# GpSimd makes one of four weight sums and the activation sums for the down projection, and two more feed-forward blocks go by seven products

## The chip, the cores and the metric

The kernel runs on one core of a Trainium2 chip. The metric is the device time of one execution in microseconds (us), less being better. The engines of the core are called here as the profile calls them: PE (TensorE, matrix products), DVE (VectorE), ACT (ScalarE), POOL (GpSimd) and SP (SyncE, whose queue issues most of the loads).

## The reference

One encoder layer over 512 tokens of width 1024, in float32: a mixer of two attention head groups, cross-attention into 256 memory tokens, and a SwiGLU feed-forward network (FFN). Only the FFN is touched:

```python
def swiglu(h, w_gate_up, w_down):
    g, u = jnp.split(h @ w_gate_up, 2, axis=-1)
    return (jax.nn.silu(g) * u) @ w_down
...
    h = rms_norm(x, g_ffn_pre[l])
    x = x + rms_norm(swiglu(h, w_gate_up[l], w_down[l]), g_ffn_post[l])
```

Here `h` is 512 x 1024, `w_gate_up` is 1024 x 5632 and `w_down` is 2816 x 1024.

## The kernel before

Every float32 matrix is split into a high part (a cast to the format `F32R` that PE takes) and a low part (the rest), and a product is made of three matmuls: high x high, high x low, low x high. Each weight tile therefore costs a cast on ACT (for weights of the FFN line 924) and a subtraction on DVE (line 925), both before PE can use it.

**Gate and up.** The 5632 columns of `w_gate_up` are 22 blocks of 256, `n` = 0 to 21. An even `n` is the gate of hidden pair `u = n // 2`, an odd one the up of the same pair. Blocks 0 and 1 use weights loaded early. A later block is a 2 x 2 arrangement of 512 x 512 by 512 x 128 quarters, and is made in one of two ways:

- by eight products (`eight_weights`, `eight`): two loads of 512 KB, `lower` and `upper`, each split; 96 matmuls of 256 columns; one evacuation per half.
- by seven products after Winograd (`seven_weights`, `seven`): 84 matmuls. The weights need four sums `s1` to `s4` of quarters (each 128 x 512), and 3.5 split tiles of 1024 in place of 2. The results come out of PSUM by five additions on DVE (lines 1161 to 1171), and for an up block two multiplications with the gate follow (lines 1181, 1183).

The split weights of a block are four items (a11; `s2`,`s4`; the raw `upper` quarters; `s3`,`s1`) in a ring in SBUF, which holds three slots of 1024 columns, so DVE and ACT prepare a block about one block ahead of PE. The raw loads have three buffers, `sums` two. Lines 951 to 954 make the sums. `EIGHT` names the blocks that go by eight.

Loads, casts, sums and evacuations stand in program order with priorities, and a scheduler in the build orders the instructions of each engine; the chip then runs each engine's queue in that order, with semaphores between engines.

**Products of the activations.** By seven products the activations need sums too, made once at the start (`f11`, `f12`, `f21`, `f22`; lines 1138 to 1142, split at 1134 and 1135 into `t1` to `t4`). Line 887 makes the low part of the activations' second half, on which the last matmuls of blocks 0 and 1 wait.

**Down.** `w_down` is taken in two column halves, in pairs `i` of 256 rows. Pairs 0 to 3 and 9, 10 are plain; pairs 4 to 8 (`SEVEN`) go by seven products, and `late_seven` makes their activation operands: first the raw quarters are split (`put`, lines 1217 and 1218), then four sums in place (lines 1222 to 1225, each 128 x 256), then the sums are split. The weights of these pairs are summed on DVE at lines 1001 to 1003.

An instruction whose two inputs both lie in SBUF is called a two-SBUF instruction below (lines 925, 951 to 954, 1222 to 1225 are such); lines 1161 to 1171 read one input from PSUM.

Of the kernel before, what the change touches and what calls it, by code (L numbers as in the profile page):

```python
# [11 lines left out]
ALU = mybir.AluOpType  # L12
AX = mybir.AxisListType

P = 128
# [21 lines left out]
def hybrid_block_kernel(  # L37
# [20 lines left out]
    act, dve, pool, pe = nc.scalar, nc.vector, nc.gpsimd, nc.tensor  # L58
# [12 lines left out]
    def f32(ap):  # L71
        return ap.bitcast(F32)
# [158 lines left out]
    with tc.tile_pool(name="mix", bufs=1, reuse_waits="tile") as bp:  # L231
# [126 lines left out]
        for t in range(NT):  # L358
# [3 lines left out]
                out=z[:, t, :], in0=acc0[t][:, 256:264], scalar=r, in1=gn[:, B_F : B_F + 8],  # L362
# [299 lines left out]
    with tc.tile_pool(name="cross", bufs=1, reuse_waits="tile") as cp:  # L662
# [20 lines left out]
        with later(-115):  # L683
            for c in range(4):
                hi, lo = unit()
                acc = bank("a")
                for b in range(2):
# [9 lines left out]
                    out=kT[:, 1, 2 * c : 2 * c + 2, :], in0=a3,  # L697
                    in1=f32(kT[:, 0, 2 * c : 2 * c + 2, :]), op=ALU.subtract,
# [7 lines left out]
        for half in range(2):  # L706
            hi, lo = unit()
            for t in range(NT):
                acc = bank("a")
                for k in range(4):  # L710
# [5 lines left out]
                    out=m, in0=acc, scalar=rs_g[1][:, t : t + 1], in1=m, op0=ALU.mult, op1=ALU.add  # L716
# [3 lines left out]
                if half:  # L720
                    r = small(1, "prs")
                    dve.scalar_tensor_tensor(
                        out=r, in0=mix_ms[:, 0, t : t + 1], scalar=EPS, in1=mix_ms[:, 1, t : t + 1],
# [4 lines left out]
                        out=mix[:, t, :], in0=mix[:, t, :], scalar=r, in1=xo[t], op0=ALU.mult, op1=ALU.add  # L728
# [39 lines left out]
        for h in range(4):  # L768
            hi, lo = unit()
            q = qq[:, h % 2]  # L770
            for b in range(2):
                acc = bank("a")
                cs = slice(b * P, (b + 1) * P)
                for k in range(KB):
# [3 lines left out]
                    out=q[:, 1, b, :], in0=acc, scalar=1.0 / 16.0, in1=f32(q[:, 0, b, :]),  # L778
# [3 lines left out]
            for i in range(0, NT, 2):  # L782
                s = bank("s")
                for j in range(2):
# [8 lines left out]
                    out=nm, in_=s.rearrange("p (j n) -> p j n", j=2), axis=AX.X, op=ALU.max, negate=True  # L793
# [9 lines left out]
                for j in range(2):  # L803
                    dve.tensor_scalar(
                        out=p[:, i + j, :], in0=p[:, i + j, :], scalar1=rs[:, j : j + 1],
# [11 lines left out]
            for b in range(2):  # L817
                acc = bank("o")
                cs = slice((2 * h + b) * P, (2 * h + b + 1) * P)
                for k in range(2):  # L820
# [6 lines left out]
                    out=oTl[2 * h + b], in0=acc, in1=f32(oTh[2 * h + b]), op=ALU.subtract  # L827
# [68 lines left out]
        def load_raw(w, k0, nkb, c0, ncol):  # L896
            raws[0] += 1
            raw = wp.tile([P, nkb, ncol], F32, tag="raw", name=f"fraw{raws[0]}", bufs=3)
            nc.sync.dma_start(
                raw, w[k0 * P : (k0 + nkb) * P, c0 : c0 + ncol].rearrange("(k p) n -> p k n", p=P)  # L900
            )
            return raw
# [13 lines left out]
        def item(at, size, fill):  # L916
            items.append((at, at + size, fill))

        def fill_from(at, shape, src, order=None):
            def fill():  # L920
                h, l = split(at, None, shape)
                h2, l2 = (a.rearrange(order) for a in (h, l)) if order else (h, l)
                v = src()
                act.copy(h2, v)  # L924
                dve.tensor_tensor(out=l2, in0=v, in1=f32(h2), op=ALU.subtract)  # L925
                return h, l

            return fill
# [3 lines left out]
        def single():  # L932
            nslot[0] += 1
            return AS_WEIGHTS + 512 * (nslot[0] % 2)

        def double():
            nslot[1] += 1
            return AS_WEIGHTS + 1024 + 1024 * (nslot[1] % 3)

        def seven_weights(n, c0):  # L940
            raw, total = {}, sums[:, n % 2]
            s2, s4, s3, s1 = (total[:, i] for i in range(4))

            def a11():
                raw["lower"] = load_raw(w_gate_up, 0, 4, c0, 256)
                raw["upper"] = load_raw(w_gate_up, 4, 4, c0, 256)
                return raw["lower"][:, :, :P]

            def s2_s4():
                lower, upper = raw["lower"], raw["upper"]  # L950
                dve.tensor_tensor(out=s1, in0=lower[:, :, P:], in1=upper[:, :, P:], op=ALU.add)
                dve.tensor_tensor(out=s2, in0=s1, in1=lower[:, :, :P], op=ALU.add)
                dve.tensor_tensor(out=s4, in0=s2, in1=upper[:, :, :P], op=ALU.add)
                dve.tensor_tensor(out=s3, in0=lower[:, :, :P], in1=lower[:, :, P:], op=ALU.add)
                return total[:, 0:2]

            two = dict(c=2, k=4, n=P)
            item(at := single(), 512, fill_from(at, dict(k=4, n=P), a11))
            item(at := double(), 1024, fill_from(at, two, s2_s4))
            item(at := double(), 1024, fill_from(at, two, lambda: raw["upper"], "p c k n -> p k c n"))  # L960
            item(at := double(), 1024, fill_from(at, two, lambda: total[:, 2:4]))
# [5 lines left out]
                    fill_from(at, dict(k=4, n=256), lambda k0=k0: load_raw(w_gate_up, k0, 4, c0, 256)),  # L967
                )

        EIGHT = (2, 3, 11)  # L970
        for n in range(2, FB):
            (eight_weights if n in EIGHT else seven_weights)(n, (n % 2) * FF + (n // 2) * 256)

# [67 lines left out]
        def hidden(u):  # L1041

            if u == 0:
                return G
            if u < 4 or u == 10:
                return U.rearrange("p t b n -> p b t n")
            if u in (4, 8):
                tag, size = {4: ("vm", 4160), 8: ("pt", 2112)}[u]
                gf.append(cp.tile([P, size], F32, tag=tag, name=f"gf{u}"))
            at = (u % 4 if u < 8 else u % 2) * 1024  # L1050
            return gf[-1][:, at : at + 1024].rearrange("p (b t n) -> p b t n", b=2, t=2)
# [53 lines left out]
        def up_eight(dst):  # L1105
            def done(m, acc):
                dve.tensor_tensor(out=dst[:, m], in0=G[:, :, m], in1=halves(acc), op=ALU.mult)

            return done

        def eight(tags, done, parts):
            accs = [bank(tag) for tag in tags]
            for half, bs in enumerate(((b11, b12), (b21, b22))):
                ((h, l),) = take()
                for m in range(2):
                    w = [a[:, :, m * P : (m + 1) * P] for a in (h, l)]
                    for n, ns in enumerate((left, right)):
                        begin = half == 0 and n == 0
                        product(accs[m][:, ns], w, bs[n], begin, half == 1 and n == 1, WHOLE if m or n or not half else parts)
                    if half:  # L1120
                        done(m, accs[m])
# [67 lines left out]
        for u in range(1, FB // 2):  # L1189
            parts = IN_STEP if u in (1, 2, 4, 6, 8, 10) else WHOLE  # L1190
            if 2 * u in EIGHT:
                eight(("a", "a"), gate_eight, parts)
            else:
                seven(G, ("a", "a", "a", "o"), gate_seven, parts)
            dst = hidden(u)
            if 2 * u + 1 in EIGHT:
                eight(("s", "s"), up_eight(dst), WHOLE)
# [13 lines left out]
        def late_seven(u):  # L1211

            h, l = late7[u]
            f = gf_views[u].rearrange("p (c n) -> p c n", n=256)

            def put(d, a):
                act.copy(h[:, d], f[:, a])
                dve.tensor_tensor(out=l[:, d], in0=f[:, a], in1=f32(h[:, d]), op=ALU.subtract)

            put(slice(0, 1), slice(0, 1))  # L1220
            put(slice(1, 3), slice(2, 4))
            dve.tensor_tensor(out=f[:, 3], in0=f[:, 1], in1=f[:, 3], op=ALU.add)
            dve.tensor_tensor(out=f[:, 1], in0=f[:, 0], in1=f[:, 1], op=ALU.subtract)
            dve.tensor_tensor(out=f[:, 0], in0=f[:, 3], in1=f[:, 0], op=ALU.subtract)
            dve.tensor_tensor(out=f[:, 2], in0=f[:, 2], in1=f[:, 0], op=ALU.subtract)
            put(slice(3, 7), slice(0, 4))

        gh, gl = ({(k if k < 8 else k + 12): a for k, a in enumerate(g)} for g in (gh, gl))
# [22 lines left out]
        for half, tail in enumerate((2, 3)):  # L1251
# [64 lines left out]
            for i in body:  # L1316
                if i in SEVEN:
                    if half == 0 and i == SEVEN[0]:
                        cuts.append(P)
                    seven_products(i, i == SEVEN[-1])  # L1320
                    if half == 0 and i == SEVEN[0]:
                        spare = cp.tile([P, 4160], F32R, tag="vm", name="latev")
                        copied = cp.tile([P, 1024], F32, tag="xp", name="f8", bufs=2)
                        act.copy(copied, gf_views[8])
                        gf_views[8] = copied
                        late(9, spare)
                        at = 2048 + AS_WEIGHTS
                        lows = cp.tile([P, 2112], F32R, tag="pt", name="latep")[:, AS_WEIGHTS:]
                        late7[8] = tuple(
                            a.rearrange("p (c n) -> p c n", n=256) for a in (spare[:, at : at + 1792], lows[:, :1792])  # L1330
                        )
                        late_seven(8)
                        gb3 = cp.tile([P, D], F32, tag="xp", name="gb3", bufs=2)
                        spare3 = cp.tile([P, D], F32, tag="xp", name="spare3", bufs=2)
                        junk3, gained = spare3[:, :512], spare3[:, 512:]
                        nc.gpsimd.dma_start(gb3, bcast(g_ffn_post))
                    if i == SEVEN[-1]:
                        gather()
                    continue
# [96 lines left out]
```

## Time and profile before

| | |
|---|---|
| runs | 774.8, 774.9 and 775.59 us, median 774.9 |
| profiled execution | span 771.6 us; its own time outside the profiler is not listed beside it, and the 3.3 us to the median lie around the span |
| PE busy | 755.6 us, 98% |
| DVE busy | 600.3 us, 78% |
| ACT busy | 429.4 us, 56% |
| POOL busy | 62.5 us, 8% |
| gate and up, blocks by seven or eight | about 442 to 649 us |
| down | about 649 to 766 us |

Busy time is the time during which at least one instruction of an engine runs. PE's matmuls overlap one another, so its pace is read from the starts of its instructions, not from their durations. The same holds in a small way for DVE, whose next instruction starts some 0.09 us before the end of the one before is recorded.

### The profile page before, as it was taken

To read this page: it belongs to the slowest core of one execution; us is meant where nothing else is said; L and a number is where in the kernel's file an instruction comes from. 1 tells how busy PE (TensorE), PEld (TensorE's weight loads), DVE (VectorE), ACT (ScalarE), POOL (GpSimd) and SP (SyncE) were. 2 spreads that over 40 slices of the span, in tenths; PEclk is the share of its full clock that TensorE was granted. 3 is DMA by queue.
4 is the path that set the end of the run, shared out by engine and by line. 5 is a ranking of instruction groups with operands and counts; after the bars stand their busy time and mean duration, and the time that the engine had idled before them with its cause. 6 is when DMAs were issued, how large, how long until landed. Compare 5 with 4: busy or idle time off the path is not lost.

```text
span 771.6 us, 12900 instructions
## 1 busy us (share of the span) xinstructions
PE 755.6 (98%) x5012; PEld 677.0 (88%) x5012; DVE 600.3 (78%) x1098; ACT 429.4 (56%) x784; POOL 62.5 (8%) x105
## 2 busy tenths in 40 slices
PE   9999999999999999999999999999999999999996
PEld 9977888887778988877778999999999999898985
DVE  8668889789886688545653779999899998987746
ACT  7558889567874457444553625554444446553421
POOL 1001132100321210000002100000000000000001
PEclk9999999999999999999999999999999999999999
DMA  7522023422313725311340202332433332233312
GB/s 273 139 70 68 28 56 97 123 82 82 109 56 112 267 98 197 120 54 56 131 143 27 83 28 83 110 110 82 138 110 110 110 110 90 102 112 108 106 59 109
DMA packets 60749, 80.05 MB, mean 104 GB/s; under 512 B 2705, under 2 KB 43665, under 8 KB 60689
## 3 DMA queue, kind: packets, MB, share of 16 engines
q1 hardware_dynamic: 59264, 74.49, 29.9%
q0 software_dynamic: 1280, 4.72, 1.7%
q8 instruction: 39, 0.64, 0.3%
q14 instruction: 22, 0.17, 0.1%
q10 hardware_dynamic: 144, 0.02, 0.0%
HBM read 77.13 MB, written 2.10 MB: 103 GB/s over the span
## 4 chain that ended last, share of the span: by engine, by line
PE 79%; DVE 9%; ACT 6%; issue 3%; DMA 2%; POOL 1%; DVEq 0%; POOLq 0%; ACTq 0%
PE ps_a L144 12%; PE ps_a L146 12%; PE ps_a L143 12%; PE ps_a L1094 3%; PE ps_a L1097 3%; PE ps_a L1095 3%; PE ps_s L1097 3%; PE ps_s L1094 3%; PE ps_s L1095 3%; PE ps_s L143 2%; PE ps_s L144 2%; PE ps_s L146 2%; PE ps_t L552 2%; PE ps_o L561 2%; PE ps_s L533 1%
## 5 line engine op out<-in xcount | busy, mean ns | idle before, releaser
L924 ACT CAST ring_hi<-fraw 128x1024 fp32r<-128x1024 f32 (+1 forms) x62 | 57.2, 932 | 61.0 <-DVE fraw L1003 17.0
L126 DVE TENSOR_TENSOR lo<-raw,hi 128x1024 fp32r<-128x1024 f32 x56 | 68.2, 1224 | 20.5 <-ACT hi L125 20.3
L925 DVE TENSOR_TENSOR ring_lo<-fraw,ring_hi 128x1024 fp32r<-128x1024 f32 (+1 forms) x62 | 66.5, 1075 | 17.4 <-ACT ring_hi L924 17.1
L146 PE MATMUL ps_a<-hTh,lo 128*128 128x512 f32 x192 | 76.6, 399 | 0.0
L144 PE MATMUL ps_a<-hTl,hi 128*128 128x512 f32 x192 | 75.9, 395 | 0.0
L143 PE MATMUL ps_a<-hTh,hi 128*128 128x512 f32 x192 | 75.8, 395 | 0.0
L125 ACT CAST hi<-raw 128x1024 fp32r<-128x1024 f32 x56 | 57.8, 1048 | 25.3 <-PE ps_a L144 21.2
L924 ACT CAST ring_hi<-sums 128x1024 fp32r<-128x1024 f32 x34 | 35.7, 1049 | 35.5 <-PE ps_t L1095 10.2
L925 DVE TENSOR_TENSOR ring_lo<-sums,ring_hi 128x1024 fp32r<-128x1024 f32 x34 | 41.4, 1219 | 2.1 <-ACT ring_hi L924 2.1
L144 PEld LDWEIGHTS ps_a<-hTl,hi 128*128 128x128 f32 x192 | 36.1, 188 | 6.4
L146 PEld LDWEIGHTS ps_a<-hTh,lo 128*128 128x128 f32 x192 | 36.1, 188 | 6.3
L143 PEld LDWEIGHTS ps_a<-hTh,hi 128*128 128x128 f32 x192 | 36.2, 188 | 5.7
L547 ACT ACTIVATE p<-p,nm 128x128 f32<-128x128 f32 (+1 forms) x64 | 36.1, 565 | 8.1 <-DVE nm L537 7.2
L1094 PE MATMUL ps_a<-b,ring_hi 128*128 128x256 f32 x140 | 39.1, 279 | 0.0
L1097 PE MATMUL ps_a<-b,ring_lo 128*128 128x256 f32 (+1 forms) x146 | 39.0, 274 | 0.0
L1095 PE MATMUL ps_a<-b,ring_hi 128*128 128x256 f32 x140 | 38.7, 276 | 0.0
L1097 PE MATMUL ps_s<-b,ring_lo 128*128 128x256 f32 x128 | 35.3, 276 | 0.0
L1095 PE MATMUL ps_s<-b,ring_hi 128*128 128x256 f32 x128 | 35.3, 276 | 0.0
L1094 PE MATMUL ps_s<-b,ring_hi 128*128 128x256 f32 x128 | 35.3, 276 | 0.0
L554 ACT CAST pth<-ps_t 128x128 fp32r<-128x128 f32 (+1 forms) x64 | 27.0, 424 | 14.5 <-PE ps_t L552 13.7
L555 DVE TENSOR_TENSOR ptl<-ps_t,pth 128x128 fp32r<-128x128 f32 (+1 forms) x64 | 30.7, 487 | 5.0 <-ACT pth L554 3.8
L552 PE MATMUL ps_t<-ident,p 128*128 128x128 f32 x160 | 28.1, 275 | 1.1 <-DVE p L549 0.8
(552 smaller groups left out, 2630.5 us busy)
## 6 DMA issues: line engine op xcount, KB each, us to landing
raw<-in_dram SPq DMA_DIRECT2D x64, 512.0 KB, 3.7
fraw<-in_dram SPq DMA_DIRECT2D x62, 512.0 KB, 3.5
cb<-in_dram SPq DMA_DIRECT2D x8, 256.0 KB, 2.5
xo<-in_dram POOLq DMA_DIRECT2D x4, 512.0 KB, 7.5
out_dram<-yd SPq DMA_DIRECT2D x8, 256.0 KB, 2.0
rawv<-in_dram SPq DMA_DIRECT2D x3, 520.0 KB, 6.5
xt<-in_dram SPq DMA_DIRECT2D x3, 512.0 KB, 6.6
gb<-in_dram POOLq DMA_DIRECT2D x3, 512.0 KB, 4.4
```

Of the source, the lines that this page charges most:

```text
L125: act.copy(hi[:, j : j + n, :], raw)
L126: dve.tensor_tensor(out=lo[:, j : j + n, :], in0=raw, in1=f32(hi[:, j : j + n, :]), op=ALU.subtract)
L143: pe.matmul(dst, sh, mh, start=first, stop=False)
L144: pe.matmul(dst, sh, ml, start=False, stop=False)
L146: pe.matmul(dst[:, to], sl, mh[:, to], start=False, stop=last)
L547: act.activation(p[:, :n], p[:, :n], AF.Exp, bias=nm, scale=-1.0, accum_out=sm)
L552: pe.transpose(tp[:, k * P : (k + 1) * P], p[:, k * P : (k + 1) * P], ident)
L924: act.copy(h2, v)
L925: dve.tensor_tensor(out=l2, in0=v, in1=f32(h2), op=ALU.subtract)
L1094: pe.matmul(dst, w[0][:, k, :], b[:, 0, k, :], start=first and k == 0, stop=False)
L1095: pe.matmul(dst, w[0][:, k, :], b[:, 1, k, :], start=False, stop=False)
L1097: pe.matmul(dst[:, to], w[1][:, k, :], b[:, 0, k, to], start=False, stop=last and k == 3)
```

## The change

Two places move additions from DVE to POOL, and `EIGHT` loses two of its three blocks.

```diff
             def s2_s4():
                 lower, upper = raw["lower"], raw["upper"]
-                dve.tensor_tensor(out=s1, in0=lower[:, :, P:], in1=upper[:, :, P:], op=ALU.add)
-                dve.tensor_tensor(out=s2, in0=s1, in1=lower[:, :, :P], op=ALU.add)
+                pool.tensor_tensor(out=s1, in0=lower[:, :, P:], in1=upper[:, :, P:], op=ALU.add)
+                dve.tensor_tensor(out=s3, in0=lower[:, :, :P], in1=lower[:, :, P:], op=ALU.add)
+                dve.tensor_tensor(out=s2, in0=s3, in1=upper[:, :, P:], op=ALU.add)
                 dve.tensor_tensor(out=s4, in0=s2, in1=upper[:, :, :P], op=ALU.add)
-                dve.tensor_tensor(out=s3, in0=lower[:, :, :P], in1=lower[:, :, P:], op=ALU.add)
                 return total[:, 0:2]
...
-        EIGHT = (2, 3, 11)
+        EIGHT = (2,)
...
             put(slice(0, 1), slice(0, 1))
             put(slice(1, 3), slice(2, 4))
-            dve.tensor_tensor(out=f[:, 3], in0=f[:, 1], in1=f[:, 3], op=ALU.add)
-            dve.tensor_tensor(out=f[:, 1], in0=f[:, 0], in1=f[:, 1], op=ALU.subtract)
-            dve.tensor_tensor(out=f[:, 0], in0=f[:, 3], in1=f[:, 0], op=ALU.subtract)
-            dve.tensor_tensor(out=f[:, 2], in0=f[:, 2], in1=f[:, 0], op=ALU.subtract)
+            pool.tensor_tensor(out=f[:, 3], in0=f[:, 1], in1=f[:, 3], op=ALU.add)
+            pool.tensor_tensor(out=f[:, 1], in0=f[:, 0], in1=f[:, 1], op=ALU.subtract)
+            pool.tensor_tensor(out=f[:, 0], in0=f[:, 3], in1=f[:, 0], op=ALU.subtract)
+            pool.tensor_tensor(out=f[:, 2], in0=f[:, 2], in1=f[:, 0], op=ALU.subtract)
             put(slice(3, 7), slice(0, 4))
```

In the changed kernel line 951 is the sum `s1` on POOL, line 952 is `s3`, 953 `s2` and 954 `s4` on DVE; so `s2` no longer reads `s1`, and the first user of `s1` is the block's last ring item. By the loop over `n` = 2 to 21, blocks by seven go from 17 to 19 (blocks 3 and 11 are added); the title of the change counts blocks 0 and 1 with them.

The order of instructions on POOL, from the last square-root step of the layer before the FFN to the end, before the change (`gb` is a load issued by POOL, `frs` the final norm):

```order
L151 TENSOR_TENSOR rs_4573<-rs_4573,mhalf 128x1
L1336 DMA gb_7389<-in_dram 128x1024
L1241 TENSOR_TENSOR frs_8055<-frs_8055,mhalf 128x1
```

and after it, at the point between the last weight sums and the first activation sums (`fraw` are raw weights, `gf` the activations of pairs 4 to 9):

```order
L951 TENSOR_TENSOR sums<-fraw_6705,fraw_6707 128x512
L951 TENSOR_TENSOR sums<-fraw_6820,fraw_6822 128x512
L951 TENSOR_TENSOR sums<-fraw_6933,fraw_6935 128x512
L1222 TENSOR_TENSOR gf_5669<-gf_5669 128x256
L1223 TENSOR_TENSOR gf_5669<-gf_5669 128x256
L1224 TENSOR_TENSOR gf_5669<-gf_5669 128x256
L1225 TENSOR_TENSOR gf_5669<-gf_5669 128x256
L1222 TENSOR_TENSOR gf_5669<-gf_5669 128x256
```

POOL had nothing between those two lines; now it has 19 sums and 20 short sums, in the order of the blocks, ahead of and around the load of `gb`.

DVE at the start of the FFN, between the two instructions of line 887, before (`f` is a quarter of the activations, line 181 its evacuation from PSUM; the sums are those of block 4):

```order
L887 TENSOR_TENSOR b_4280<-f_4577,b_4280 128x1024
L181 TENSOR_SCALAR f_4578<-ps_t_4599,gn 128x256
L181 TENSOR_SCALAR f_4578<-ps_t_4608,gn 128x256
L951 TENSOR_TENSOR sums<-fraw_4914,fraw_4916 128x512
L181 TENSOR_SCALAR f_4578<-ps_t_4608,gn 128x256
L952 TENSOR_TENSOR sums<-sums,fraw_4914 128x512
L887 TENSOR_TENSOR b_4280<-f_4578,b_4280 128x1024
```

and after (the sums are those of block 3, the last of them of block 4):

```order
L887 TENSOR_TENSOR b_4280<-f_4577,b_4280 128x1024
L952 TENSOR_TENSOR sums<-fraw_4630 128x512
L181 TENSOR_SCALAR f_4578<-ps_t_4599,gn 128x256
L953 TENSOR_TENSOR sums<-sums,fraw_4632 128x512
L181 TENSOR_SCALAR f_4578<-ps_t_4608,gn 128x256
L954 TENSOR_TENSOR sums<-sums,fraw_4632 128x512
L181 TENSOR_SCALAR f_4578<-ps_t_4608,gn 128x256
L952 TENSOR_TENSOR sums<-fraw_4978 128x512
L887 TENSOR_TENSOR b_4280<-f_4578,b_4280 128x1024
```

Four sums now stand between the two, where two stood; on PE the first matmul that waits for the second line 887 stands 41 instructions behind the one that waits for the first, where it stood 31 behind.

DVE over one block in the steady part, before (here `s1` at line 951; the sums of one block are made while the raw `upper` quarters of the block ahead of it are split):

```order
L951 TENSOR_TENSOR sums<-fraw_6352,fraw_6354 128x512
L954 TENSOR_TENSOR sums<-fraw_6352 128x512
L925 TENSOR_TENSOR ring_lo<-sums,ring_hi 128x1024
L1161 TENSOR_TENSOR G<-ps_a_6231,v 128x512
L952 TENSOR_TENSOR sums<-sums,fraw_6352 128x512
L1162 TENSOR_TENSOR G<-ps_a_6232,G 128x256
L953 TENSOR_TENSOR sums<-sums,fraw_6354 128x512
L925 TENSOR_TENSOR ring_lo<-fraw_6239,ring_hi 128x4x2x128
L1167 TENSOR_TENSOR G<-ps_a_6230,G 128x256
L1169 TENSOR_TENSOR G<-ps_o_6233,G 128x256
L1171 TENSOR_TENSOR G<-ps_o_6233,G 128x512
L925 TENSOR_TENSOR ring_lo<-sums,ring_hi 128x1024
```

and after:

```order
L925 TENSOR_TENSOR ring_lo<-fraw_6362,ring_hi 128x512
L952 TENSOR_TENSOR sums<-fraw_6362 128x512
L953 TENSOR_TENSOR sums<-sums,fraw_6364 128x512
L925 TENSOR_TENSOR ring_lo<-sums,ring_hi 128x1024
L1161 TENSOR_TENSOR G<-ps_a_6241,v 128x512
L954 TENSOR_TENSOR sums<-sums,fraw_6364 128x512
L1162 TENSOR_TENSOR G<-ps_a_6242,G 128x256
L925 TENSOR_TENSOR ring_lo<-fraw_6249,ring_hi 128x4x2x128
L1167 TENSOR_TENSOR G<-ps_a_6240,G 128x256
L1169 TENSOR_TENSOR G<-ps_o_6243,G 128x256
L1171 TENSOR_TENSOR G<-ps_o_6243,G 128x512
L925 TENSOR_TENSOR ring_lo<-sums,ring_hi 128x1024
```

One addition has gone from DVE's block, and the rest keeps its place.

## The prediction, made before the changed kernel had run

> **What bounds the kernel now.** I read the page's head first, then busy time in stretches of 10 us, then the starts of instructions within a block, then PE's waits.
>
> ```profile
> span 771.6 us, 12900 instructions
> PE 755.6 (98%) x5012; PEld 677.0 (88%) x5012; DVE 600.3 (78%) x1098; ACT 429.4 (56%) x784; POOL 62.5 (8%) x105
> ```
>
> PE is busy throughout, so over the whole span it is the bound. The shares hide what each stage does:
>
> ```profile
> core 0: us, PE busy (x) PEld busy (x) DVE busy (x) ACT busy (x) POOL busy (x), PEclk, DMA share, GB/s
> 440.00:450.00 10.00, 9.94 (x85) 9.69 (x83) 9.27 (x15) 3.50 (x8) 0.00 (x0) 1.00 0.04 12
> 450.00:460.00 10.00, 10.00 (x90) 10.00 (x89) 5.54 (x7) 3.08 (x5) 0.00 (x0) 1.00 0.17 54
> 460.00:470.00 10.00, 10.00 (x90) 10.00 (x90) 9.97 (x10) 6.22 (x8) 0.00 (x0) 1.00 0.17 52
> 550.00:560.00 10.00, 10.00 (x91) 10.00 (x90) 7.87 (x12) 2.99 (x4) 0.00 (x0) 1.00 0.35 108
> 600.00:610.00 10.00, 10.00 (x91) 10.00 (x90) 9.76 (x15) 5.28 (x9) 0.00 (x0) 1.00 0.35 108
> ```
>
> From 450 on PE never stops, but DVE is nearly full too where blocks go by seven (9.76 of 10), and has room where they go by eight (5.54, 7.87). How far DVE is ahead is read from the last weight split of a block (line 925 from `sums`) and the first matmul that uses it, for block 4 and then for two blocks six apart:
>
> ```profile
> 469.80 1.22 DVE L925 TENSOR_TENSOR ring_lo<-sums,ring_hi 128x1024 fp32r<-128x1024 f32 x1
> 570.08 1.22 DVE L925 TENSOR_TENSOR ring_lo<-sums,ring_hi 128x1024 fp32r<-128x1024 f32 x1
> 629.23 1.22 DVE L925 TENSOR_TENSOR ring_lo<-sums,ring_hi 128x1024 fp32r<-128x1024 f32 x1
> 477.08 0.28 PE L1094 MATMUL ps_a<-thi,ring_hi 128*128 128x256 f32 x1
> 573.89 0.28 PE L1094 MATMUL ps_a<-thi,ring_hi 128*128 128x256 f32 x1
> 631.26 0.28 PE L1094 MATMUL ps_a<-thi,ring_hi 128*128 128x256 f32 x1
> ```
>
> The lead (PE's start less DVE's end) is 477.08 − 471.02 = 6.1 us at block 4, 573.89 − 571.30 = 2.6 and 631.26 − 630.45 = 0.8 at the others. Between those two DVE takes 59.15 / 6 = 9.86 us a block and PE 57.37 / 6 = 9.56, or 0.1134 us for each of its 506 matmuls (six blocks of 84, and two pieces that a split adds). So a row of blocks by seven costs DVE 0.3 us of lead each, and eight-product blocks pay the lead back. Whoever lowers DVE's block below 9.56 can do without them; whoever raises it makes DVE the bound.
>
> **The change, part by part.** *Two blocks by seven:* 2 × 12 matmuls fewer, 24 × 0.1134 = −2.7 us of PE. This counts only while DVE keeps up.
>
> *One sum fewer in DVE's block.* The rows of a block, with the load that its `upper` buffer then takes:
>
> ```profile
> 598.91 0.69 DVE L952 TENSOR_TENSOR sums<-sums,fraw 128x512 f32<-128x512 f32 x1
> 599.51 1.22 DVE L925 TENSOR_TENSOR ring_lo<-sums,ring_hi 128x1024 fp32r<-128x1024 f32 x1
> 600.65 0.69 DVE L1161 TENSOR_TENSOR G<-ps_a,v 128x512 f32<-128x512 f32 x1
> 601.25 0.68 DVE L953 TENSOR_TENSOR sums<-sums,fraw 128x512 f32<-128x512 f32 x1
> 601.85 0.42 DVE L1162 TENSOR_TENSOR G<-ps_a,G 128x256 f32<-128x256 f32 x1
> 602.18 1.22 DVE L925 TENSOR_TENSOR ring_lo<-fraw,ring_hi 128x1024 fp32r<-128x1024 f32 x1
> 603.43 0.37 SPq L899 DMA_DIRECT2D fraw<-in_dram  x1
> DMA to landing us min/median/max: 3.4/3.4/3.5
> ```
>
> Start to start a 128x512 sum takes 0.60 us, some 0.12 more where the next reads its result: I take 0.66 saved a block. What POOL does with the sum no row shows in the FFN. How the two engines get on when both read two inputs from SBUF, earlier rows show:
>
> ```profile
> L581 POOL TENSOR_TENSOR sq<-sq,o x6: 1289/1292/2301, 109.4 to 243.8; 128x512 f32<-128x512 f32 x6
> 241.57 1.22 DVE L126 TENSOR_TENSOR lo<-raw,hi 128x1024 fp32r<-128x1024 f32 x1
> 241.74 1.95 POOL L580 TENSOR_TENSOR o<-o 128x512 f32<-128x512 f32 x1 [16.35 <-DVE ol L574]
> 207.23 1.29 POOL L620 TENSOR_TENSOR msq<-msq 128x512 f32<-128x512 f32 x1 [0.74 <-ACT msq L618]
> 208.12 1.48 DVE L126 TENSOR_TENSOR lo<-raw,hi 128x1024 fp32r<-128x1024 f32 x1 [0.76 <-ACT hi L125]
> 129.77 1.04 POOL L580 TENSOR_TENSOR o<-o 128x512 f32<-128x512 f32 x1 [2.48 <-DVE rc L548]
> 130.04 0.69 DVE L555 TENSOR_TENSOR ptl<-ps_t,pth 128x512 fp32r<-128x512 f32 x1
> ```
>
> Alone, POOL takes 1.29 us for a product of two 128x512 inputs, or 1.04 for line 580. At 241.74 it took 0.91 longer than that, as if it began at 242.65, 1.08 after DVE's two-SBUF instruction. At 208.12 it was DVE that took 1.48 instead of 1.22, as if it began 0.14 before POOL's end at 208.52. A DVE instruction with one input from PSUM, at 130.04, kept its 0.69 under a POOL sum. So each waits for the other's whole instruction when both have two SBUF inputs. The Trainium skill says the same more sharply (SBUF — State Buffer, "Who interferes with whom"): the pair of ports is an exclusive lock, whoever issues first has it for the whole instruction, and a DVE instruction with two SBUF inputs contends with a GpSimd instruction that reads SBUF. By that rule the forecast's sum below stands as it is; without any lock POOL's sums would be free, and the terms of the start, of gate and up and of down would fall away, leaving −2.7 us. What it leaves open, who wins when DVE's next instruction is already queued, no row here shows either.
>
> When does POOL's sum become ready? The load issues at 603.43, behind the split at 602.18, and lands 3.4 us later at 606.8. Until line 1161 of the next block at some 610.5 DVE runs two-SBUF instructions alone. So POOL meets them in each block. If it gets in at the boundary between two of them, as 1.08 against DVE's own pitch of 1.14 suggests, DVE loses b = 1.08 + 1.29 − 0.14 − 1.14 = 1.09 us a block, and has saved 0.66. If POOL is kept out until line 1161, which reads PSUM and lasts 0.60 to the next sum, DVE loses 1.29 − 0.14 − 0.60 = 0.55. Lower bound 0 (POOL always under PSUM instructions), upper 1.29 (POOL's whole duration). I take 1.09, by the only rows that show POOL pending. DVE breaks even with PE at 9.86 − 0.66 + b = 9.56, b = 0.36, or 0.56 if I count the 0.2 us of each block in which DVE is idle (9.76 busy of 10).
>
> At b = 1.09 a block is 9.86 − 0.66 + 1.09 − 0.2 = 10.09 us, 0.53 over PE's. Over the 18 blocks 4 to 21, all by seven, 9.5 us. The products with the gate that DVE also makes in few of these blocks (line 1063, 1.13 each, two of them) add 2.3. Against them stands the lead at block 4: 6.1 now, less 6.2 because block 3 by seven costs DVE so much more (3.5 weight splits and three or four sums for two splits, 4.2, and some 2 in evacuation), less 1.4 (12 matmuls that PE no longer spends), plus 0.66 saved, plus 3 of the 4.5 us in which DVE is idle from 450 to 460: 2.2. Gate and up: +9.5 + 2.3 − 2.2 = +9.6.
>
> *The start.* Two matmuls wait for line 887, just in time:
>
> ```profile
> 442.86 1.22 DVE L887 TENSOR_TENSOR b<-f,b 128x1024 fp32r<-128x1024 f32 x1
> 446.40 1.22 DVE L887 TENSOR_TENSOR b<-f,b 128x1024 fp32r<-128x1024 f32 x1
> 444.12 0.38 PE L144 MATMUL ps_a<-b,gate_w 128*128 128x256 f32 x1
> 447.76 0.40 PE L144 MATMUL ps_a<-b,gate_w 128*128 128x256 f32 x2
> ```
>
> Between the two lines 887 stand two sums more now (2 × 0.6 = 1.2 us), and PE reaches the second wait ten instructions later (10 × 0.1134 = 1.1). Uncovered, 0.1; with one block of b by block 3's `s1`, up to 1.1. I take 0.9, since DVE is full there (9.27).
>
> *The sums for down.*
>
> ```profile
> PE ps_s L144 <- DVE ring_lo L925: 1.1, 2, 0.6
> 667.01 0.42 DVE L1224 TENSOR_TENSOR gf<-gf 128x256 f32<-128x256 f32 x1
> 667.35 0.42 DVE L1222 TENSOR_TENSOR gf<-gf 128x256 f32<-128x256 f32 x1
> L151 POOL TENSOR_TENSOR rs<-rs,mhalf 128x1 f32<-128x1 f32 x4 | 2.2, 542 | 13.8 <-DVE rs L150 13.8
> L1336 POOL DMA_DIRECT2D gb<-in_dram x1: 573/573/573, 658.3 to 658.3; - x1
> L1370 DVE TENSOR_TENSOR yd<-yd,gb x4: 691/692/693, 702.9 to 710.8; 128x512 f32<-128x512 f32 x4
> ```
>
> In the down stage PE waits for DVE twice, 1.1 us in all: the most that can be won. DVE gives up 20 sums of 0.34, 6.8 us. POOL needs between 0.54 (a column of one) and 1.29 for one; I estimate 0.75. DVE's splits and weight sums around them have two SBUF inputs and can lose about 0.75 − 0.2 = 0.55 to each, 11 − 6.8 = +4.2 at worst. Where between −1.1 and +4.2: a loss counts only where PE has caught up with DVE, and it does so at two of some ten places; I take +1.0. POOL's load of `gb` now stands behind eight of these sums. It was issued at 658.3 and is first used at 702.9, so the 44 us between cover it; it could cost something only if the eight sums ended after 698.
>
> **Sum:** −2.7 + 0.9 + 9.6 + 1.0 = +8.8. The profiled span would go from 771.6 to 780.4, and the median, 3.3 us above the span, from 774.9 to **783.7**.
>
> **Rivals.**
> *POOL waits until DVE's run ends (the other side).* Two-SBUF instructions of DVE overlap at their seams (1.22 long, 1.14 apart), so the ports may never come free within a run. Then b = 0.55 or less, below 0.56: PE stays the bound, gate and up add 0, the start 0 to 0.4, down −1.1 to +1.0: −3.8 to −1.3, middle about −2.3, **772.6 us**. For it: at 241.74 and in the 2301 ns of line 581 it is POOL that waited, and DVE kept 1.22. Against: no row shows POOL held past the end of one DVE instruction. It decides at b = 0.56.
> *Half of it:* POOL meets the run in some blocks only, b near 0.65, 18 × 0.1 = 1.8 more: −2.7 + 0.9 + 1.8 + 0 to 1 = 0 to +1.0, **775 us**.
> *Only the down stage loses:* gate and up hold, but chains of four sums on POOL (3 us against 1.4) come late and DVE loses 0.55 to most: −2.7 + 0.9 + 4.2 = +2.4, **777.5 us**. For it: DVE is nearly full just where PE waits:
>
> ```profile
> 680.00:690.00 10.00, 8.95 (x76) 8.56 (x75) 8.97 (x16) 5.22 (x7) 0.00 (x0) 1.00 0.18 58
> ```
>
> **Chances and range.** The runs before spread by 0.8 us; about 0.2%, 1.55 us, can be told from no change. Forecast 0.42, POOL waiting 0.33, half 0.13, down alone 0.12. Faster 0.33, same 0.13, slower 0.42 + 0.12 = 0.54. The range goes from 771.8 (most of the faster case) to 788.5: the forecast with down at its worst (+3.2) and half of the idle 0.2 a block not absorbed (+1.6). The forecast's own range is 778 to 788.5.
>
> **What would show it.** POOL's line 951 longer than 1.29 in most blocks means that it waits for DVE; lines 925 and 952 to 954 longer than 1.22 and 0.69 mean that DVE waits for POOL, and their excess in a block is b. In the forecast PE waits from about block 7 on before lines 1094 to 1097, with DVE's `ring_lo` as the releaser, some 0.5 us a block; in the rival it has none, and the row of PE starts from 450 to 649 is 2.7 us shorter. The start shows at PE's second wait, between 447.8 and 450, and down in PE's waits from 649 on, 1.1 us before. I am wrong if DVE's pitch of a block by seven falls below 9.56.

## The result, and the profile after

The changed kernel takes 795.75 us (median of 5 runs, 795.18 to 796.83) against 774.83 (774.29 to 775.59) for the kernel before: ratio 1.0272, 95% interval 1.026 to 1.0285, 20.9 us slower. Slower was forecast; 783.7 was too small by 12 us, and the time lies above the range.

The head of the page of the changed kernel:

```profile
span 795.0 us, 12937 instructions
PE 764.1 (96%) x4988; PEld 680.9 (86%) x4988; DVE 616.6 (78%) x1081; ACT 430.6 (54%) x790; POOL 114.8 (14%) x144
```

PE does 24 matmuls fewer and is recorded busy longer. Stretches of 10 us of the changed kernel, of gate and up (the first three) and of down (the last two), in the columns PE, PEld (weight loads), DVE, ACT, POOL, the granted clock of PE as a share of full speed, and DMA:

```profile
core 0: us, PE busy (x) PEld busy (x) DVE busy (x) ACT busy (x) POOL busy (x), PEclk, DMA share, GB/s
490.00:500.00 10.00, 10.00 (x91) 10.00 (x90) 9.86 (x15) 5.82 (x10) 1.48 (x1) 1.00 0.33 103
500.00:510.00 10.00, 8.75 (x77) 8.55 (x76) 9.97 (x13) 4.28 (x5) 1.44 (x1) 1.00 0.34 107
600.00:610.00 10.00, 9.71 (x85) 9.51 (x85) 9.79 (x14) 4.01 (x5) 1.36 (x1) 1.00 0.33 105
680.00:690.00 10.00, 8.65 (x60) 7.83 (x58) 3.74 (x3) 2.45 (x3) 6.85 (x7) 1.00 0.17 54
690.00:700.00 10.00, 6.94 (x39) 6.34 (x40) 5.69 (x9) 4.37 (x8) 3.91 (x4) 0.83 0.13 36
```

Up to 500 PE is full, and from there on it waits in nearly each block while DVE is full with fewer instructions (13 or 14, 15 before). In down PE and DVE are idle at the same time, and from 680 to 690 POOL is busier than DVE and ACT. PE's first matmul of gate and up (line 143, from `gate_w`) starts at 428.72 (427.68 before), its first of down at 661.82 (648.94), its last at 787.59 (764.12). So gate and up, with the start, lost 233.10 − 221.26 = 11.8 us and down 125.77 − 115.18 = 10.6; 1.0 us more lies ahead of the feed-forward network, which the change leaves alone. (These are two single executions, with spans 23.4 us apart where the medians differ by 20.9. The times of the runs lie 1.7 to 1.8 us above their spans, so the profiled execution of the kernel before took some 773.3 us, 1.5 less than its median; the 3.3 us that stand ahead of the prediction as lying around the span are made of these two.)

**Gate and up.** The groups of PE's waits, with us in total, times and the longest, then two groups of DVE and the sums on POOL (busy us, mean ns of one), then the rows of one block, all of the changed kernel:

```profile
PE ps_s L1097 <- DVE ring_lo L925: 5.5, 7, 1.3
PE ps_a L1097 <- DVE ring_lo L925: 2.5, 6, 0.9
PE ps_a L144 <- DVE b L887: 0.8, 1, 0.8
```

```profile
L951 POOL TENSOR_TENSOR sums<-fraw,fraw 128x512 f32<-128x512 f32 x19 | 31.4, 1652 | 172.8 <-DMA fraw<-in_dram 108.7 <-DVE ring_lo L925 30.9 <-DVE sums L952 26.7
L925 DVE TENSOR_TENSOR ring_lo<-fraw,ring_hi 128x512 fp32r<-128x512 f32 x19 | 20.7, 1090 | 0.2 <-ACT ring_hi L924 0.2
L953 DVE TENSOR_TENSOR sums<-sums,fraw 128x512 f32<-128x512 f32 x19 | 20.4, 1073 | 1.2 <-DMA fraw<-in_dram 0.9
```

```profile
580.29 1.22 DVE L925 TENSOR_TENSOR ring_lo<-sums,ring_hi 128x1024 fp32r<-128x1024 f32 x1
597.69 0.68 DVE L925 TENSOR_TENSOR ring_lo<-fraw,ring_hi 128x512 fp32r<-128x512 f32 x1
597.91 1.62 POOL L951 TENSOR_TENSOR sums<-fraw,fraw 128x512 f32<-128x512 f32 x1 [7.93 <-DVE sums L952]
598.29 1.79 DVE L953 TENSOR_TENSOR sums<-sums,fraw 128x512 f32<-128x512 f32 x1
642.99 1.22 DVE L925 TENSOR_TENSOR ring_lo<-sums,ring_hi 128x1024 fp32r<-128x1024 f32 x1
```

POOL's sum becomes ready at 597.91 while DVE runs a two-SBUF split, and takes 0.33 us longer than its 1.29. DVE's next sum takes 1.79 instead of 0.69, 1.10 more. The means 1090 and 1073, against 0.69 us for the same sizes before, say that it is mostly these two lines that POOL meets. Between 580.29 and 642.99 lie six blocks: 10.45 us a block, 9.86 before.

**Down.** Pieces of the chain that ended last, in order of time (start us, us, what), then the rows of DVE and of PE at its end:

```profile
678.17 1.79 POOL gf L1222
680.03 1.61 POOL gf L1223
...
686.54 0.75 POOL gf L1225
687.31 1.06 ACT latelo L1217
688.39 1.24 DVE latelo L1218
...
690.60 0.92 ACT ring_hi L995 x2
```

```profile
684.38 1.48 DVE L1218 TENSOR_TENSOR latehi<-gf,latehi 128x1024 fp32r<-128x1024 f32 x1 [3.35 <-ACT latehi L1217]
691.05 0.38 PE L143 MATMUL ps_s<-ring_hi,latex 128*128 128x256 f32 x1 [2.40 <-ACT ring_hi L995]
```

The sums of two pairs run on POOL from 678.17 to 687.29, 9.1 us, one after the other. ACT's casts and DVE's splits of the sums wait for them in order; behind these, on ACT, stand the weights of the next pair (line 995), and PE waits for those. DVE itself is idle for 3.35 us there.

After two such waits close together (2.40 us, then 0.90) the granted clock falls. Stretches of 1 us of the changed kernel:

```profile
692.00:693.00 1.00, 0.66 (x3) 0.66 (x4) 1.00 (x3) 0.34 (x1) 0.00 (x0) 0.74 0.00 0
693.00:694.00 1.00, 1.00 (x7) 1.00 (x6) 1.00 (x3) 0.00 (x0) 0.00 (x0) 0.50 0.00 0
694.00:695.00 1.00, 1.00 (x7) 1.00 (x7) 1.00 (x3) 0.00 (x0) 0.16 (x1) 0.50 0.00 0
695.00:696.00 1.00, 1.00 (x6) 0.93 (x5) 0.10 (x1) 0.82 (x1) 0.92 (x2) 0.55 0.00 0
```

At 0.74, 0.50, 0.50 and 0.55 these four cost 1.7 us, and the same happens from 706 to 710 (0.57, 0.50, 0.50, 0.72). Of the 10.6 us of down, 7.1 − 1.1 = 6.0 are more of PE's waits, 3.4 the clock; the other 1.2 were not followed. By the Trainium skill (TensorE: Matmul & The Clock Gate, Part 1) the clock halves after an idle window of some 3.4 us and needs one of activity to return; the trace agrees on the half and on 3.4 us of it, though PE's gaps were only 2.4 and 0.9 us here, and 1.0 and 0.9 the second time.

### The profile page after: what moved, and what is told of

Read it like the earlier page. It is cut to its first block, busy times and chain, and to the rows that moved or that the text cites. A ratio compares the mean times of both kernels' runs of the same rounds, so it can differ in the third digit from the quotient of the medians.

```text
span 795.0 us, 12937 instructions
## 1 busy us (share of the span) xinstructions
PE 764.1 (96%) x4988; PEld 680.9 (86%) x4988; DVE 616.6 (78%) x1081; ACT 430.6 (54%) x790; POOL 114.8 (14%) x144
## 4 chain that ended last, share of the span: by engine, by line
PE 60%; DVE 20%; ACT 7%; issue 6%; DMA 3%; POOL 3%; SPq 0%; DVEq 0%; POOLq 0%; ACTq 0%
PE ps_a L144 12%; PE ps_a L146 12%; PE ps_a L143 11%; DVE ring_lo L925 7%; PE ps_t L552 2%; PE ps_s L144 2%; PE ps_s L146 2%; PE ps_s L143 2%; DVE sums L953 2%; DMA fraw<-in_dram 2%; PE ps_o L561 1%; PE ps_s L533 1%; PE ps_s L534 1%; DVE sums L952 1%; PE ps_a L1097 1%
## 5 line engine op out<-in xcount | busy, mean ns | idle before, releaser
L925 DVE TENSOR_TENSOR ring_lo<-fraw,ring_hi 128x1024 fp32r<-128x1024 f32 (+1 forms) x62 | 73.1, 1186 | 20.1 <-ACT ring_hi L924 20.1
L126 DVE TENSOR_TENSOR lo<-raw,hi 128x1024 fp32r<-128x1024 f32 x56 | 68.2, 1223 | 20.7 <-ACT hi L125 20.4
L951 POOL TENSOR_TENSOR sums<-fraw,fraw 128x512 f32<-128x512 f32 x19 | 31.4, 1652 | 172.8 <-DMA fraw<-in_dram 108.7
L925 DVE TENSOR_TENSOR ring_lo<-sums,ring_hi 128x1024 fp32r<-128x1024 f32 x38 | 47.3, 1244 | 0.0
L924 ACT CAST ring_hi<-sums 128x1024 fp32r<-128x1024 f32 x38 | 39.8, 1047 | 13.1 <-PE ps_a L1095 5.4
L1176 ACT ACTIVATE G<-G 128x256 f32<-128x256 f32 x36 | 14.1, 414 | 47.9 <-DVE G L1161 31.3
L1097 PEld LDWEIGHTS ps_a<-b,ring_lo 128*128 128x128 f32 x146 | 27.0, 188 | 0.0
```

Of the source, the lines that this page charges most:

```text
L126: dve.tensor_tensor(out=lo[:, j : j + n, :], in0=raw, in1=f32(hi[:, j : j + n, :]), op=ALU.subtract)
L1097: pe.matmul(dst[:, to], w[1][:, k, :], b[:, 0, k, to], start=False, stop=last and k == 3)
```

## Experiments

Theory: GpSimd's sum costs DVE 1.1 us a block and saves 0.6, so DVE becomes the bound of gate and up; and in down the sums make a chain that others wait for in order. Rivals: the missing blocks by eight make the loss; PE loses in down because it has no lead left.

### Parts undone, parts alone

`x1`: the changed kernel, lines 1222 to 1225 back on DVE.

```diff
-            pool.tensor_tensor(out=f[:, 3], in0=f[:, 1], in1=f[:, 3], op=ALU.add)
+            dve.tensor_tensor(out=f[:, 3], in0=f[:, 1], in1=f[:, 3], op=ALU.add)
...
```

> The changed kernel with the four activation sums of each down pair back on VectorE. Theory (the down loss is made in the down stage itself, by chains of four sums on GpSimd with ACT's casts and VectorE's splits waiting in order behind them): the time from the first down matmul to the last falls from 125.8 to about 115.2 us, the granted clock stays at 1.00 there, gate and up stay as long as in the changed kernel, median 795.8 - 10 = 786 us. Rival (PE enters the down stage without a lead, and that costs the 10 us whoever sums): 793 to 796 us.

786.04 us, ratio to the kernel before 1.0155 (1.014 to 1.017). Down took 115.6 us again, gate and up stayed (233.4 us from the first matmul to down, 233.1 in the changed kernel). The down loss is made by these sums.

`x2`: the changed kernel, the four weight sums as before.

```diff
-                pool.tensor_tensor(out=s1, ...)
...
+                dve.tensor_tensor(out=s1, in0=lower[:, :, P:], in1=upper[:, :, P:], op=ALU.add)
...
```

> The changed kernel with all four weight sums back on VectorE in their old order; blocks 3 and 11 still go by seven, the sums for down stay on GpSimd. Theory (GpSimd's sum costs VectorE 1.1 us a block and saves 0.6): VectorE's pitch of a block falls from 10.48 back to 9.86 us, gate and up gain 8 to 9 us, down stays at about 125.8: 787 us. Rival (the two eight-product blocks that are gone cost the most): 793 to 796 us.

788.59 us, 1.0186 (1.0169 to 1.0203). Down's first matmul starts 661.82 − 653.96 = 7.9 us earlier; 0.7 of them lie ahead of the first matmul of gate and up (428.01, 428.72 in the changed kernel), so gate and up gained 7.1. Down stays long (124.4 us).

`x3`: the kernel before with only

```diff
-        EIGHT = (2, 3, 11)
+        EIGHT = (2,)
```

> The kernel before with blocks 3 and 11 by seven products and nothing on GpSimd. Theory: 24 matmuls fewer, -2.7; VectorE's block is 0.3 us over PE's, 18 x 0.33 = 5.9, and 2.3 for the products kept, less 1.5 of lead at block 4: PE waits 6.7 us, sum +4.0: 778.8 us (776 to 781). Rival (these blocks are the main loss of gate and up, +12): 786 us. Third (PE keeps its lead): 772.1 us.

779.41 us, 1.0068 (1.0053 to 1.0083), as the theory has it. DVE at 9.86 us a block cannot feed PE, which needs 9.53 (84 matmuls at 0.1134), without the two blocks by eight.

`x4`: the kernel before with only the weight sums of the changed one.

> The kernel before with the sum s1 on GpSimd and the changed order of the sums; blocks 2, 3 and 11 by eight, the sums for down on VectorE. Theory (+0.6 us of VectorE a block, 10.48 against PE's 9.53): 17 blocks x 0.95 = 16, less the leads of 6.1 at block 4 and some 5 after block 11: +5 to +7, 781 us. Rival (the loss needs the eight-product blocks gone): 775 us or less, VectorE's instructions no longer than before.

777.37 us, 1.0044 (1.0029 to 1.0059): slower, but +3.3 and not +5 to +7. After block 11 DVE's pitch was 10.25 us (seven blocks), not 10.48, and the three blocks by eight paid most of it back. Each part alone costs (5.3 and 3.3), and both together 12.0 (`x1`): the blocks by eight were what paid for a slower DVE.

### Reads of SBUF, or the wait for the result?

`x5`: as `x1`, but POOL writes zeros to `s1`.

```diff
-                pool.tensor_tensor(out=s1, in0=lower[:, :, P:], in1=upper[:, :, P:], op=ALU.add)
+                pool.memset(s1, 0.0)
```

> The changed kernel with the sums for down on VectorE, and with GpSimd filling s1 with zeros instead of adding: it writes the same 128x512 in SBUF but reads nothing there (the sum itself is left out). Theory (VectorE waits for GpSimd's reads): no VectorE instruction of lines 925 and 952 to 954 is longer than 1.22 and 0.69, its block takes 9.86 - 0.6 + 0.1 = 9.35 us, below PE's 9.53, PE is the bound from block 4 on, 774.1 - 2.7 + 1 at the start = 772.4 us. Rival (the changed order, with each sum waiting for the one before, or the blocks 3 and 11 by seven make the loss): 779 us or more.

770.81 us, 0.995 (0.9933 to 0.9967). PE never waits in gate and up. The same two groups of DVE in `x5`:

```profile
L925 DVE TENSOR_TENSOR ring_lo<-fraw,ring_hi 128x512 fp32r<-128x512 f32 x19 | 13.0, 685 | 0.2 <-ACT ring_hi L924 0.2
L953 DVE TENSOR_TENSOR sums<-sums,fraw 128x512 f32<-128x512 f32 x19 | 13.1, 688 | 0.3
```

20.7 and 20.4 us have become 13.0 and 13.1, with the same order of instructions and one write of the same size on POOL. A fill is shorter than a sum (0.53 us against 1.29), but length alone does not do it either: in `x13` below, fills run on POOL for 8.6 us without a break, and DVE's splits beside them keep their lengths (line 925 at 666.46 takes 1.22, line 996 at 668.66 0.68). The time is GpSimd's reads. And with the order of the changed kernel but no reads, DVE takes 9.3 us a block (six blocks between its splits of `s2`, `s4` at 549.31 and 604.96).

`x7`: the kernel before, and POOL adds the same two quarters once more into a spare row.

```diff
+                pool.tensor_tensor(out=rrow..., in0=lower[:, :, P:], in1=upper[:, :, P:], op=ALU.add)
                 dve.tensor_tensor(out=s1, in0=lower[:, :, P:], in1=upper[:, :, P:], op=ALU.add)
```

> The kernel before, VectorE making all four weight sums, with one addition of the same two quarters more on GpSimd in each block by seven; nobody reads its result. Theory (the ports): VectorE loses 1.1 us in most blocks and saves nothing, 9.86 + 1.1 = 10.96 us against PE's 9.53 over 17 blocks, 24 less 11 of lead: +13 us, 787 us (783 to 791). Rival (ACT and VectorE wait for GpSimd's result, and the ports cost little): 774 to 776 us.

789.54 us, 1.0185 (1.0162 to 1.0209). Nobody waits for the result, and 14.8 us are lost. Together with `x5` this shows that in gate and up it is GpSimd's reads beside DVE that cost the time, not the wait for its result.

### The sums for down

`x14`, run later, shows them alone (the kernel before, lines 1222 to 1225 on POOL):

> The kernel before with the four activation sums of each down pair on GpSimd and nothing else changed. The down loss of the changed kernel, alone: 774.9 + 9.7 = 784.6 us (782 to 787), in the runs of VectorE waiting 2 to 3 us for GpSimd's chain with the next pairs' weights behind it in its order. If it only comes together with the losses of gate and up: 775 to 778 us.

787.53 us, 1.0164 (1.0147 to 1.0181): they cost here 12.7 us alone, more than the 782 to 787 expected. Down took 127.2 us, 12.0 more than before: 5.9 are more of PE's waits (7.0 against 1.1), and some 6 the clock, which was at half while PE was busy for 12.3 us. How PE's waits fall together thus sets a good part of the price.

`x6`: the kernel before, and behind each pair's sums on DVE four additions on POOL that nobody reads.

```diff
             dve.tensor_tensor(out=f[:, 2], in0=f[:, 2], in1=f[:, 0], op=ALU.subtract)
+            for _ in range(4):
+                pool.tensor_tensor(out=rrow[:, 0:256], in0=f[:, 0], in1=f[:, 2], op=ALU.add)
```

> The kernel before, VectorE making all its sums, with four additions of 128x256 more on GpSimd behind the activation sums of each down pair; nobody reads their results. Theory (in the down stage it is the length of the chain on GpSimd, with ACT and VectorE waiting in order, and not the ports): VectorE loses up to 0.55 to some of the 20, PE has slack in most places, 774 to 777 us. Rival (the ports): VectorE and PE lose about what the change lost there, 782 to 785 us.

785.04 us, 1.0134 (1.0117 to 1.015): against the theory. Rows of `x6`:

```profile
660.38 6.68 POOL L1227 TENSOR_TENSOR rrow<-gf 128x256 f32<-128x256 f32 x1
662.96 0.42 DVE L1218 TENSOR_TENSOR latehi<-gf,latehi 128x256 fp32r<-128x256 f32 x1
663.63 1.22 DVE L1218 TENSOR_TENSOR latex<-gf,latex 128x1024 fp32r<-128x1024 f32 x1
670.85 0.80 POOL L1227 TENSOR_TENSOR rrow<-gf 128x256 f32<-128x256 f32 x1
671.72 0.80 POOL L1227 TENSOR_TENSOR rrow<-gf 128x256 f32<-128x256 f32 x1
670.09 0.96 DVE L1224 TENSOR_TENSOR gf<-gf 128x256 f32<-128x256 f32 x1
670.97 0.95 DVE L1222 TENSOR_TENSOR gf<-gf 128x256 f32<-128x256 f32 x1
```

Two things show here. The first addition takes 6.68 us: it is kept out for some 5.9 us while DVE runs eleven instructions at their usual lengths (two of them stand above), and the same happens at 692.20 (6.11 us). From 667 on the engines take turns where both are back to back: POOL's additions of 0.80 us start 0.87 apart, and DVE's sums take 0.96 instead of 0.42. Which of the two happens when both want to read is not explained by any run here. DVE loses about 9 us in this way (eighteen instructions, most of them by 0.53), so reads alone can cost down this much.

`x9`, `x11`, `x13`: the kernel before, the four sums of a pair replaced by fills with zeros.

```diff
-            dve.tensor_tensor(out=f[:, 3], in0=f[:, 1], in1=f[:, 3], op=ALU.add)
...
+            for _ in range(16):
+                pool.memset(f[:, 3], 0.0)
```

(`x13`; two fills of each of the four quarters in `x9`, four in `x11`.)

> The kernel before with the four activation sums of each down pair replaced by eight fills with zeros on GpSimd, in the same place of the chain (the sums are left out): some 3 us a group as with the sums, but nothing read from SBUF. Theory (in the changed kernel it is the wait for GpSimd's chain, in order ahead of ACT's casts and VectorE's splits, that makes PE wait in the down stage): most of the loss stays, 781 to 785 us, and no VectorE instruction there is longer than in the kernel before. Rival (VectorE waiting for GpSimd's reads makes the loss): 774 us or a little less, since VectorE has 6.8 us less to do.

> As the run with eight fills in place of the four activation sums, but with sixteen: eight took 2.0 us a group (0.255 each), where the sums of the changed kernel took 4.0 to 5.1; sixteen should take 4.1 us, and still read nothing from SBUF (the sums are left out). Theory (the length of GpSimd's chain makes PE wait): 780 to 784 us, with PE waiting some 6 us in the down stage. Rival (only the ports do): 773 us, as with eight.

> The kernel before with the four activation sums of each down pair replaced by sixteen fills of one quarter, the one that the sums write first: they all wait for the split of that quarter and run one after the other, 4.1 us a group and 8.2 for two groups, as long as the changed kernel's sums took (9.1 for two), and read nothing from SBUF (the sums are left out). In the run before, fills of other quarters ran ahead, and two groups took 4.1 together. Theory (the length of GpSimd's chain makes PE wait): 780 to 785 us, with ACT and VectorE idle for 3 us at a time behind the chain. Rival (only the ports do): 773 us again.

772.96 us (0.9976, 0.9966 to 0.9986), 773.27 (0.9981, 0.997 to 0.9992) and 775.11 (0.9997, 0.9988 to 1.0007). Rows of `x13`:

```profile
664.06 8.63 POOL L1223 MEMSET gf<- 128x256 f32 x32 [2.35 <-DVE latehi L1218]
671.73 1.05 ACT L1217 CAST latehi<-gf 128x1024 fp32r<-128x1024 f32 x1 [3.96 <-POOL gf L1223]
```

ACT waits 3.96 us behind a chain of 8.6 us for two pairs, and PE loses nothing. But the build, which counts such fills as long, had put one more pair's weights (lines 996 to 1003) ahead of the waiting splits on DVE. So a chain costs nothing where the next weights are ahead of it, or it is the reads. `x15` and `x16` kept the reads: the sums on POOL, and sixteen or eight fills of the last quarter behind them (the last sum is lost). In `x15` the next pair's weights stand ahead of the waiting splits as in `x13`; in `x16` one of their two casts on ACT, and DVE's lines 1002 and 1003, stand behind the first of them.

> The sums on GpSimd as in the run above, followed in each group by sixteen fills of the last quarter (which the last sum wrote, so that its result is lost). GpSimd's chain is then longer, 3.2 to 4.6 us of sums and 4.1 of fills, its reads of SBUF are the same, but the build, which counts the fills as long, puts the next pairs' weights (lines 996 to 1003) ahead of the splits that wait for the chain, on ACT and on VectorE. Theory (what costs PE is the order: weights behind splits that wait for GpSimd): 775 to 778 us in spite of the longer chain. Rival (the ports, or the length of the chain as such): 784 us or more.

> The same with eight fills a group: some 2 us of fills behind the sums, and one pair's weights, not all, ahead of the splits. Order theory: 775 to 780 us. Rival: 784 us or more.

789.44 us (1.0188, 1.0173 to 1.0203) and 786.67 (1.0153, 1.0138 to 1.0168). Order alone does not save it. But the chain of two pairs had become 16.3 and 12.6 us long in these runs, more than the 9.1 of the changed kernel and the 8.6 of `x13` (in `x15` PE then waits 8.4 us for a cast of further weights, line 924, that stands behind the sums' casts), so that they don't part reads from length. That stays open: whether down would hold with the sums on POOL, a chain of 9 us and the weights ahead was not tried. What the trace of the changed kernel shows is the path: DVE's instructions of 655 to 712 are longer by only some 1.4 us in all, while it and ACT sit idle behind the chain; and the chain is itself longer by the contention, 9.1 us for eight sums that take 0.74 alone and start 0.8 apart (1.6 to 1.8 for three of them that run beside DVE's splits, 2.8 us more).

### A version that beats both

`x8`: the kernel before with `EIGHT = (2, 3)`.

> The kernel before with block 11 by seven and blocks 2 and 3 still by eight. Theory: 12 matmuls fewer, -1.4; VectorE's lead, 3.5 to 4 us where the ring is full, falls by 0.33 in each of the ten blocks 11 to 20 and by 1.1 where a product is kept, and just about lasts: 0 to 1.5 us of waits, 772.7 to 774.2 us. Rival (the lead of block 11 is needed in full): 3 us of waits or more, 776 us.

774.95 us, 1.0009 (1.0 to 1.0019): no gain. One block by eight is worth its 1.4 us of PE.

`x10`: the changed kernel with the sums for down on DVE, and `s1` added on the way from memory.

```diff
+                for k0, op in ((0, ALU.bypass), (4, ALU.add)):
+                    nc.gpsimd.dma_start(
+                        s1,
+                        w_gate_up[k0 * P : (k0 + 4) * P, c0 + P : c0 + 2 * P].rearrange("(k p) n -> p k n", p=P),
+                        accum_op=op,
+                    )
...
-                pool.tensor_tensor(out=s1, in0=lower[:, :, P:], in1=upper[:, :, P:], op=ALU.add)
```

> The changed kernel with the sums for down on VectorE, and s1 made on the way from memory: GpSimd's queue loads one quarter into s1 and then loads the other onto it with an add, so that neither GpSimd nor VectorE reads SBUF for it. Theory (only GpSimd's reads cost VectorE): VectorE's block takes 9.35 us as with the fills, 770 to 773 us. Rival (the accumulating loads come late, or GpSimd's making of their descriptors and VectorE get in each other's way): more than 775 us, with ACT's casts of the sums waiting for these loads.

771.53 us, 0.9959 (0.9946 to 0.9972): faster than both kernels. The loads, one of DVE's sums, and PE's only wait from 430 us on, in `x10`:

```profile
L948 POOL DMA_DIRECT2D sums<-in_dram x38 | 39.1, 1028 | 154.7 <-DVE ring_lo L925 86.2 <-DMA sums<-in_dram 61.5 <-ACT b L179 7.0
L958 DVE TENSOR_TENSOR sums<-sums,fraw 128x512 f32<-128x512 f32 x19 | 13.1, 689 | 5.8 <-DMA fraw<-in_dram 5.5
PE ps_s L144 <- DVE ring_lo L925: 0.8, 1, 0.8
```

DVE's sums keep 689 ns, and PE does not wait in gate and up, as with the fills. This is what the change was one step from: the sum off DVE, and no addition on GpSimd beside it.

`x12`: `x10` with `EIGHT = ()`.

> The kernel with s1 made by accumulating loads, and block 2 by seven products as well (no block by eight). If PE stays the bound: 12 matmuls fewer, -1.4, 770.2 us. If the start cannot take it (block 2's four splits and three sums and the activations' sums have to be ready when PE leaves block 1): 773 us or more.

784.56 us, 1.0129 (1.0107 to 1.0151): PE waits 10.6 us at the start for the split of the activations' sums. Block 2 by eight covers that.

## Why the prediction was right and wrong

- **The ports, b = 1.09 us.** Right in kind: 1.10 in the rows above, 18.4 us over 19 blocks in the five groups of lines 925 and 952 to 954 (0.97 a block), and by `x5` and `x7` the reads are the cause. In 17 of the 19 blocks POOL gets in at DVE's next boundary or sooner, though DVE's instructions overlap there; in two (472.80, 482.79) it lets one more pass. So the rival in which it is kept out of DVE's run did not hold for gate and up, but it does occur: in `x6` twice, for more than 5 us.
- **DVE's block, 10.09 us.** Mis-sized: 10.45. I took off 0.2 for idle time that does not shrink (9.79 us busy of 10 from 600 to 610, 9.76 before). The rest is what the reads cost from start to start: against the 9.3 of `x5`, with the same order and no reads, they add some 1.2, not 1.09, and the sum taken away saves some 0.6, not 0.66. Part of the difference to the 0.97 is that an instruction behind a wait no longer starts before the end of the one ahead (line 953 at 577.86 takes 1.79, and the next starts at 579.68). The new order is not the reason: by `x5` the block has it without loss, and in the kernel before three dependent sums already started 0.72 apart in some blocks (607.37, 608.09, 608.81).
- **The lead and the start.** PE began to wait at 508, near block 7, as forecast, but by luck in part: the lead at block 4 was 477.88 − 474.46 = 3.4 us and not 2.2, and the larger loss of each block used it up. (The splits by which the lead was read are those of `s2`, `s4`, the second of a block's four items and not its last.) The start cost 0.8 us (0.9 forecast). Gate and up with the start came to +11.8, where −2.7 + 0.9 + 9.6 = 7.8 was forecast.
- **Down, +1.0 with +4.2 as the upper end.** This step failed, and it is the larger part of the miss: +10.6, so 9.6 of the 14.6 us by which the spans (23.4 apart) missed the sum of 8.8; gate and up make 4.0 and the time ahead of the network 1.0. The step took the cost to be DVE's time beside POOL's reads, and only where PE had caught up. It left out what is queued on ACT and DVE behind a split that waits for a chain of eight sums on a slower engine, and the half clock after PE's waits (3.4 us). My estimate of 0.75 us for one sum was right (0.74); eight of them one after the other, with ACT, DVE and the next weights in order behind them, were the point. That the sums on POOL make the loss is shown (`x1`, `x14`); the way through the queues is read from the trace, and how much of it is the reads and how much the length of the chain stays open. The rival "only the down stage loses" named these chains, but priced them at 4.2 by DVE's time alone, two fifths of the loss, and had gate and up hold.
- **24 matmuls, −2.7 us.** They are saved, and show only where DVE keeps up (`x5`, `x10`).

## What to carry to other kernels

Before a sum is moved to GpSimd, ask what runs on VectorE at the moment its inputs land: where VectorE runs instructions with two SBUF inputs back to back, a moved 0.6 us cost it 1.1 to 1.2 here. A move that shortens one engine's work but lengthens a chain through three engines has to be priced by what stands in the queues behind the chain's users too: in down DVE's own instructions grew by 1.4 us, and PE lost 10.6. Where an operand comes from memory anyway, an accumulating load can make the sum without slowing VectorE (`x10`: its sums stayed at 689 ns).

## What the runs showed of the hardware

GpSimd's fills (0.53 us for 128x512, 0.30 for 128x256) leave VectorE's 128x512 instructions at 0.69. By the Trainium skill (SBUF — State Buffer, "Who interferes with whom") VectorE with two SBUF inputs contends with a GpSimd instruction that reads SBUF and not with one that only writes it; `x5` and `x7` agree. Who gets in first when both engines are queued differs: GpSimd's sum mostly at VectorE's next boundary in gate and up, but in `x6` only after 5.9 us of VectorE's instructions. Two waits of PE close together (2.4 and 0.9 us, or 1.0 and 0.9), and in `x7` a single one of 3.5, were followed by some 3.4 us at half clock and so cost 1.7 us more, while the single waits of up to 1.3 us in gate and up left the clock at 1.00.
